# A transformer block kernel: eight modulation blocks on VectorE, two routing operations moved, three idle products

## The chip, the cores and the metric

The kernel runs on one core of a Trainium2 chip, in one launch. The time is the device time of that core in microseconds (us), as the median of several runs. TensorE (PE) multiplies matrices and writes PSUM; VectorE (DVE), ScalarE (ACT) and GpSimd (POOL) do the elementwise work; SyncE (SP) issues most of the transfers (DMA). Each engine works through its own queue in order.

## What is computed

Two transformer blocks, one behind the other, on 256 tokens of 1024 channels, in float32. The first takes its shifts, scales and gates from a conditioning row `c`; its token mixer adds three branches (attention, gated linear attention, Hyena), and its second half is a mixture of 16 experts. Cut to what matters here:

```
shift1, scale1, gate1, shift2, scale2, gate2 = split(silu(c) @ w_mod + b_mod, 6)
h = modulate(rms_norm(x), shift1, scale1)
m = sigmoid(g_hy) * (y_hy @ w_br_hy) + sigmoid(g_gla) * (y_gla @ w_br_gla) \
  + sigmoid(g_att) * (y_att @ w_br_att)
x = x + gate1 * (m @ w_out)
h = modulate(rms_norm(x), shift2, scale2)
scores = sigmoid(h @ router_w); sel = scores + router_b
...   # the best group of four experts by its two best, two experts in it
x = x + gate2 * grouped_moe(h)
```

`w_mod` has 1024 rows and 6 x 1024 columns. The change concerns how `gate1` and `shift2` are computed.

## The kernel before

**Weights.** They come from memory in the fixed order of `stream_order` (L249), about 1 MB at a time, into tiles `raw`; `load` (L512, L515) issues the transfers on SP as tiles come free. For most products a weight is split into a rounded high half, made by ACT, and the rest, the low half, made by DVE (`split`, L463, which writes `w`), both in the fast format fp32r; the product is then the sum of three matmuls (`mm3`). Tiles of 8 KB per partition, `raw`, `w` and `acc` of the change among them, share 19 buffers. `stream` keeps about three such halves ahead of the place where the next is taken.

**Order.** The program writes out each engine's order by hand. Beside the main line run side jobs (`Side`, L383): attention (`att`), gated linear attention (`glj`), Hyena (`hyj`) are generators, and `side.tick()` runs their next step when a planner's clock says that its operands are ready. That clock (`Clocked`, L341) adds a cost to PE, ACT or DVE for each call, so work that is added to or taken from an engine moves the steps behind it. All calls go through `Clocked.call`, so the profile gives them one line, L379.

**The modulation blocks.** `w_mod` comes in blocks of 128 rows by 2048 columns. Eight of them (shift and scale of the first half) are multiplied early; the other sixteen, blocks 0 to 15 in this document, are spread over the three branches. `mod_block` (L1354) is called in the loop over the gates of a branch (`w_brg`, four weights, each taken in two halves of 24 matmuls) and in the one over its projection (`w_br_...`). Blocks 0 to 3 lie in the gates of attention, 4 to 7 in its projection, 8 to 13 in the linear attention stage, 14 and 15 in the gates of Hyena. Blocks 0 to 7 add up to `gate1` and `shift2`, 8 to 15 to `scale2` and `gate2`. `mod_rows` (L815) multiplies a block with `cs`, which is `silu(c)` in the first of 32 columns and zero in the others, by four float32 matmuls (two instructions each) that write four groups of 32 rows of one PSUM bank `mod`:

```
for j in range(4):
    P.matmul(ps[32 * j:32 * j + 32], cs[:, k], w[:, 0, j * 512:j * 512 + 512], start=k == 0, stop=k == 7)
```

At a half's fifth block a tile `bm` is cleared by DVE and filled with `b_mod` by four transfers on ACT's queue; at its eighth, DVE adds the bank to it. The generator `mod_spread` (L1389) then splits it into `mrow`, spreads each row over the 128 partitions with eight matmuls against `pick` (32 rows), and ACT copies the results into `mod2`. For the first half it also turns `shift2` with eight transposes (`turned_half`) and multiplies it with the router's weights (`shifted`). One step of it is made in each of the next blocks.

**The attention steps** on PE turn the weights of the softmax (`c_base,e`), make the next scores (`kT,qT`) and weigh the values (`pT,kv`); ACT copies `pT` and makes `e`, DVE makes the maxima `nb`, scales `e` and makes the low half of the result `ya`. `uc` are the columns of Hyena's short convolution, of which each has an ACT and a DVE operation.

**Routing** (from L1575). When `w_out` has been multiplied, the second half's input `h` is made for two tiles of 128 tokens. `high(m)` rounds it on ACT into `h2H`, `low(m, n)` takes the rest into `h2L`, in halves of 512 columns: for the first tile on DVE, for the second on POOL, right behind `high(1)`. DVE meanwhile makes `sel`, and by comparisons (`ge`, `gt`, `cnt`, `top`, `gs`, `cg`) the `mask` of experts. Four products of `mask` (eight instructions) count tokens per expert; `residual(i)` puts `x1` into four banks `pa` by a product with the identity matrix (`c_base` in the rows). The largest count, `mosti`, is loaded by all engines for a branch (L1695, L1696) that is not taken in these runs. Behind it `gather` makes the one-hot matrix `dp` and collects the experts' tokens, from `h2H` and then `h2L`. The stage of the experts follows.

Of the kernel before, what the change touches and what calls it, by code (L numbers as in the profile page):

```python
# [18 lines left out]
D = 1024  # L19
# [400 lines left out]
def program(ctx, tc, A, out, dump=None):  # L420
# [929 lines left out]

    acc2, mod2, spreads = {}, [], []

    def mod_block(i):

        hf, k = divmod(i, 8)
        w = take("mod2", i)
        if hf:
            next(spreads[0], None)
        if k == 0:
            acc2[hf] = PS("mod")  # L1360
        mod_rows(w, k, acc2[hf])
        if k == 4:
            st["bm"] = bm = T([128, 512], "bm", tag="u4")
            V.memset(bm, 0.0)
            for j in range(4):
                S.dma_start(bm[32 * j:32 * j + 1], A["b_mod2"][:, hf * 2048 + j * 512:hf * 2048 + j * 512 + 512])
        if k == 7:
            bm = st["bm"]
            V.tensor_tensor(bm, acc2.pop(hf), bm, op=OP.add)
            spreads.append(mod_spread(st.pop("bm")))  # L1370
            if False:
                next(spreads[hf])

# [10 lines left out]
    def logits(ts, ps, start, stop):  # L1384

        for k in range(8):
            P.matmul(ps, ts[k // 4][:, k % 4 * 128:k % 4 * 128 + 128], rw[:, k], start=start and k == 0, stop=stop and k == 7)

    def mod_spread(rows):  # L1389

        rH, rL = T2([128, 512], "mrow")
        split(rH, rL, rows)
        yield
        for a in range(2):
            t = T([128, D], "mod2")
            for n in range(2):
                ps = PS()
                q = slice(32 * (2 * a + n), 32 * (2 * a + n) + 32)
                P.matmul(ps, pick[q], rH[q], start=True, stop=False)
                P.matmul(ps, pick[q], rL[q], start=False, stop=True)  # L1400
                S.activation(t[:, n * 512:n * 512 + 512], ps, AF.Copy)
            mod2.append(t)
        yield
        if len(mod2) == 2:
            ts = [turned_half(mod2[1], k4) for k4 in range(2)]
            yield
            ps = PS()
            logits(ts, ps[:, :16], True, True)
            st["shifted"] = T([128, 16], "shifted", tag="uh")
            V.tensor_copy(st["shifted"], ps[:, :16])  # L1410

    msum = mH = mL = None
# [133 lines left out]

    def low(m, n, eng=V):
        c = slice(n * 512, n * 512 + 512)
        eng.tensor_tensor(h2[1][:, m, c], h2s[m][:, c], h2[0][:, m, c], op=OP.subtract)

# [20 lines left out]
    for i in range(1, 3):  # L1571
        residual(i)
    low(0, 0)
    h2H, h2L = h2
# [14 lines left out]
    high(1)  # L1589
    for n in range(2):  # L1590
        low(1, n, G)
    sel = R(E3, "sel")
# [103 lines left out]
    with tc.If(full > CAP, label="full"):  # L1696
# [11 lines left out]
        for e in range(N_EXP):  # L1708
# [27 lines left out]
            for m in range(2):  # L1736
                for n in range(2):
                    V.tensor_tensor(hfs[m], gu[n, m], gate2[:, n * 512:n * 512 + 512], op=OP.mult)
                    P.matmul(pa[m][n], ident, hfs[m], start=False, stop=False)

    next(first)
    next(first)
# [4 lines left out]
    gated, hids, done = {}, {}, {}  # L1747
    low, high = slice(0, 64), slice(64, 128)

# [9 lines left out]
    def gate_up(e, i, ps):  # L1759

        w = take("moe_gu", 4 * e + i)
        for k in range(2):
            x = xgs[e // 4][i // 2][:, (2 * i + k) % 4, e % 4]
            for a, q in enumerate((low, high)):
                P.matmul(ps[q], x, w[k][:, a * 512:a * 512 + 512], start=i + k == 0, stop=i + k == 4)
# [17 lines left out]
    def down(g):  # L1783
# [7 lines left out]
        for i in range(2):  # L1791
            if not (last and i):
                ws = [take("moe_down", 4 * g + 2 * a + i) for a in range(2)]
            for k, n in ((k, n) for n in range(2) for k in range(2)) if last and i else ((k, n) for k in range(2) for n in range(2)):
                if last and i and not k:
                    wn = take("moe_down", 4 * g + 1 + 2 * n)
                for a, q in enumerate((low, high)):
                    w = wn[a][:, k * 512:k * 512 + 512] if last and i else ws[a][k][:, n * 512:n * 512 + 512]
                    P.matmul(ps[n][q], hid[:, a, 2 * i + k], w, start=i + k == 0, stop=i + k == 2)
# [562 lines left out]
```

## Time and profile before

| | |
|---|---|
| median of 3 runs | 1410.7 us (1408.94 to 1415.88) |
| profiled execution | 1408.6 us, its span 1406.8 us |
| busy, share of span | PE 97%, DVE 60%, ACT 45%, POOL 1% |
| granted TensorE clock, mean | 0.993 |
| transfers | 297.4 MB, 211 GB/s over the span |

The profile is of one execution. Busy times are sums over instructions; matmuls are pipelined and overlap, so the time of a group is read from the starts of the groups around it. PEclk is the granted share of PE's full clock. An idle time stands before the instruction that ended it, with what released it.

### The profile page before, as it was taken

The page shows a single profiled execution, that of the slowest core. Times are in us where ns is not written, and L with a number is a line of the kernel's source. Part 1 is how long each engine was busy: PE and PEld are TensorE (multiplying, and loading weights), DVE is VectorE, ACT ScalarE, POOL GpSimd, SP SyncE. Part 2 cuts the span into 40 slices and gives each one's busy share as a digit, 9 for nine tenths or more (in the row PEclk, how much of TensorE's full clock was granted, in tenths as well). Part 3 has the DMA queues.
Part 4 walks back from the last instruction along what each step waited for, and adds up shares of the span by engine and source line. Part 5 has one row for each costly group of instructions (what it writes and reads, how often), then busy time and mean ns, then how long its engine had stood idle before and what let it go on. Part 6 is the DMA issues. An engine that isn't in the chain of part 4 may idle for free.

```text
span 1406.8 us, 20329 instructions
## 1 busy us (share of the span) xinstructions
PE 1359.7 (97%) x8270; PEld 1056.6 (75%) x8270; DVE 839.6 (60%) x1515; ACT 632.6 (45%) x1013; POOL 8.3 (1%) x15
## 2 busy tenths in 40 slices
PE   5999999999999899999999999999999998999998
PEld 2678889878797444343488689999978887999996
DVE  4777457445876511111365885666676788566675
ACT  4643465634433311111257644555435663555541
POOL 0000000000000000000000000000000000000000
PEclk9999999999999999999999999999999999999999
DMA  9523344635469799999842355556453354555630
GB/s 372 225 71 120 150 150 150 242 134 180 170 211 359 288 422 420 421 421 421 342 180 90 120 175 185 180 180 214 176 175 125 128 180 150 180 180 183 220 136 30
DMA packets 44481, 297.40 MB, mean 211 GB/s; under 512 B 5171, under 2 KB 6371, under 8 KB 10017
## 3 DMA queue, kind: packets, MB, share of 16 engines
q1 hardware_dynamic: 41868, 291.02, 55.3%
q10 hardware_dynamic: 1924, 3.27, 0.7%
q0 software_dynamic: 592, 1.79, 0.5%
q8 instruction: 66, 1.08, 0.3%
q14 instruction: 31, 0.25, 0.0%
HBM read 295.00 MB, written 1.05 MB: 210 GB/s over the span
## 4 chain that ended last, share of the span: by engine, by line
PE 56%; DVE 6%; ACT 2%; issue 1%; ACTq 0%; DVEq 0%
PE ps L379 47%; PE pd L379 8%; DVE w L379 2%; PE pa L379 1%; DVE v L379 1%; ACT pe L379 1%; DVE rs L379 1%; PE oc L379 1%; DVE xL L379 0%; DVE sm L379 0%; PE pq L379 0%; ACT w L379 0%; DVE bs L379 0%; DVE rsa L379 0%; ACT xH L379 0%
## 5 line engine op out<-in xcount | busy, mean ns | idle before, releaser
L379 DVE TENSOR_TENSOR w<-raw,w 128x1024 fp32r<-128x1024 f32 (+3 forms) x301 | 346.2, 1195 | 82.8 <-ACT w L379 82.1
L379 ACT ACTIVATE w<-raw 128x1024 fp32r<-128x1024 f32 (+3 forms) x301 | 293.1, 1032 | 17.2 <-PE ps L379 9.9
L379 PE MATMUL ps<-xH,w 128*128 128x256 f32 x1408 | 256.5, 283 | 0.3 <-ACT xH L379 0.3
L379 PEld LDWEIGHTS ps<-xH,w 128*128 128x128 f32 x1408 | 220.6, 192 | 1.5 <-ACT xH L379 0.8
L379 PE MATMUL ps<-xL,w 128*128 128x256 f32 x704 | 199.3, 283 | 1.1 <-DVE xL L379 1.1
L379 PE MATMUL ps<-w,xH 128*128 128x512 f32 (+2 forms) x544 | 150.3, 362 | 2.6 <-ACT xH L379 2.1
L379 PEld LDWEIGHTS ps<-xL,w 128*128 128x128 f32 x704 | 134.9, 192 | 2.2 <-DVE xL L379 1.5
L379 PE MATMUL pd<-w,fh 128*128 128x512 f32 x528 | 125.6, 394 | 0.0
L379 PE MATMUL ps<-raw,xg 128*64 128x512 f32 x512 | 120.0, 600 | 0.0
L379 PE MATMUL ps<-hH,w 128*128 128x256 f32 (+1 forms) x608 | 115.7, 287 | 0.0
L379 PEld LDWEIGHTS pd<-w,fh 128*128 128x128 f32 x528 | 98.2, 188 | 21.6
L379 PEld LDWEIGHTS ps<-w,xH 128*128 128x128 f32 x544 | 95.3, 189 | 18.0 <-ACT xH L379 4.0
L379 PEld LDWEIGHTS ps<-hH,w 128*128 128x128 f32 (+1 forms) x608 | 94.9, 187 | 7.9 <-issue 2.7
L379 PE MATMUL ps<-w,xL 128*128 128x512 f32 (+2 forms) x272 | 97.8, 359 | 1.9 <-DVE xL L379 1.8
L379 PE MATMUL ps<-w,hH 128*128 128x512 f32 (+1 forms) x288 | 88.1, 390 | 0.0
L379 PE MATMUL ps<-hL,w 128*128 128x256 f32 (+1 forms) x304 | 85.9, 282 | 0.0
L379 PEld LDWEIGHTS ps<-raw,xg 128*64 128x64 f32 x512 | 33.3, 136 | 55.7 <-issue 52.6
L379 DVE SCALAR_TENSOR_TENSOR fc<-ps,par,fc 128x255 f32<-128x255 f32 x88 | 42.5, 483 | 51.8 <-ACT fc L379 50.2
L379 ACT ACTIVATE fc<-ps,par 128x256 f32<-128x256 f32 x44 | 24.8, 564 | 92.5 <-PE ps L379 66.6
L379 PEld LDWEIGHTS ps<-w,hH 128*128 128x128 f32 x288 | 52.2, 188 | 13.8 <-issue 2.7
L379 PEld LDWEIGHTS ps<-w,xL 128*128 128x128 f32 x272 | 51.3, 188 | 11.9 <-DVE xL L379 5.0
L379 PE MATMUL ps<-raw,hid 128*64 128x512 f32 x256 | 57.4, 593 | 0.1
(443 smaller groups left out, 1845.5 us busy)
## 6 DMA issues: line engine op xcount, KB each, us to landing
raw<-in_moe_gu SPq DMA_DIRECT2D x63, 1024.0 KB, 14.3
raw<-in_moe_down SPq DMA_DIRECT2D x32, 1024.0 KB, 13.5
raw<-in_mod SPq DMA_DIRECT2D x24, 1024.0 KB, 5.0
raw<-in_ffn_gate SPq DMA_DIRECT2D x22, 1024.0 KB, 4.8
raw<-in_ffn_up SPq DMA_DIRECT2D x22, 1024.0 KB, 5.0
raw<-in_ffn_down SPq DMA_DIRECT2D x22, 1024.0 KB, 4.9
raw<-in_w_brg SPq DMA_DIRECT2D x12, 1024.0 KB, 5.9
raw<-in_ple_gate SPq DMA_DIRECT2D x8, 1024.0 KB, 5.6
```

The costliest lines, as they stand in the source:

```text
L379: return f(*args, **kw)
```

## The change

Three things are changed.

1. Blocks 0 to 7 are added up on DVE. A tile `acc` of 128 x 2048 is cleared by DVE, its first row filled with `b_mod` by one transfer on ACT's queue, and for each block two operations add `raw` times the column of `cs`, 1024 columns each. `mod_sums` then splits `acc` into two pairs of `mrow` tiles and sums over the partitions with eight matmuls against `ones` (128 x 128, made once by ACT), which also spread the sum. Its steps, the turning of `shift2` and `shifted` among them, are made in blocks 8 to 13. The bank `mod` and `bm` of the first half fall away.
2. `low(1, n)` goes from POOL to DVE, and behind the branch.
3. Three products of `ident` and `x1` into a bank `idle` that nobody reads stand on PE between `residual(2)` and the products of `mask`.

The new names `left` and `right` for two slices change nothing.

```diff
+    ones = T([128, 128], "pick", F32R)
+    S.activation(ones, C("ones16"), AF.Copy, scale=16.0)
...
         w = take("mod2", i)
-        if hf:
-            next(spreads[0], None)
+        if not hf:
+
+            if k == 0:
+                st["acc"] = acc = T([128, 2048], "acc")
+                V.memset(acc, 0.0)
+                S.dma_start(acc[0:1], A["b_mod2"][:, :2048])
+            acc = st["acc"]
+            for n in range(2):
+                c = slice(n * 1024, n * 1024 + 1024)
+                V.scalar_tensor_tensor(acc[:, c], w[:, 0, c], cs[:, k, 0:1], acc[:, c], op0=OP.mult, op1=OP.add)
+            if k == 7:
+                spreads.append(mod_sums(st.pop("acc")))
+            return
+        next(spreads[0], None)
         if k == 0:
             acc2[hf] = PS("mod")
         mod_rows(w, k, acc2[hf])
...
+    def mod_sums(acc):
+
+        for a in range(2):
+            rH, rL = T2([128, D], "mrow")
+            split(rH, rL, acc[:, a * D:a * D + D])
+            yield
+            t = T([128, D], "mod2")
+            for n in range(2):
+                ps = PS()
+                for r in (rH, rL):
+                    P.matmul(ps, ones, r[:, n * 512:n * 512 + 512], start=r is rH, stop=r is rL)
+                S.activation(t[:, n * 512:n * 512 + 512], ps, AF.Copy)
+            mod2.append(t)
+            yield
+        ts = [turned_half(mod2[1], k4) for k4 in range(2)]
+        yield
+        ps = PS()
+        logits(ts, ps[:, :16], True, True)
+        st["shifted"] = T([128, 16], "shifted", tag="uh")
+        V.tensor_copy(st["shifted"], ps[:, :16])
...
-    def low(m, n, eng=V):
+    def low(m, n):
         c = slice(n * 512, n * 512 + 512)
-        eng.tensor_tensor(h2[1][:, m, c], h2s[m][:, c], h2[0][:, m, c], op=OP.subtract)
+        V.tensor_tensor(h2[1][:, m, c], h2s[m][:, c], h2[0][:, m, c], op=OP.subtract)
...
     for i in range(1, 3):
         residual(i)
+
+    idle = PS("idle")
+    for i in range(3):
+        P.matmul(idle, ident, x1[:, 0, :512], start=True, stop=True)
     low(0, 0)
...
     high(1)
-    for n in range(2):
-        low(1, n, G)
...
+    for n in range(2):
+        low(1, n)
     next(first)
     next(first)
```

**Order on DVE in the gates of attention, at the first block.** `w` are low halves of weights, `nb` and `ya` belong to an attention step. Before:

```order
L379 TENSOR_TENSOR w_1326<-raw_1262,w_1326 128x1024
L379 TENSOR_TENSOR w_1354<-raw_1262,w_1354 128x1024
L379 TENSOR_TENSOR ya_1417<-ps_1412,ya_1417 128x256
L379 TENSOR_REDUCE nb_1420<-ps_1404 128x1
...
L379 TENSOR_REDUCE nb_1423<-ps_1408 128x1
```

With the change:

```order
L379 TENSOR_TENSOR w_1328<-raw_1264,w_1328 128x1024
L379 TENSOR_TENSOR w_1356<-raw_1264,w_1356 128x1024
L379 MEMSET acc_1361 128x2048
L379 SCALAR_TENSOR_TENSOR acc_1361<-raw_990,cs_105,acc_1361 128x1024 x2
L379 TENSOR_TENSOR w_1393<-raw_1366,w_1393 128x1024
L379 TENSOR_TENSOR ya_1446<-ps_1441,ya_1446 128x256
L379 TENSOR_REDUCE nb_1449<-ps_1433 128x1
```

The memset and two products now stand between two low halves, and one more low half comes before the attention step.

**Order on PE at the end of attention.** `pT,kv` weighs the values, `c_base,e` turns the softmax, `ya,w` is the projection, `mod` a block. Before:

```order
L379 MATMUL ps_2118<-c_base_80,e_1894 128x128 x4
L379 MATMUL ps_2124<-c_base_80,e_1897 128x128 x4
L379 MATMUL ps_2130<-pT_2001,kv_592 128x256 x4
L379 MATMUL ps_2147<-hH_315,w_1973 128x256
...
L379 MATMUL ps_2207<-pT_2117,kv_592 128x256 x4
L379 MATMUL ps_2214<-ya_1417,w_2060 128x256 x6
...
L379 MATMUL ps_2214<-ya_2135,w_2088 128x256 x6
L379 MATMUL mod_1359<-raw_1941,cs_105 32x512 x4
```

With the change:

```order
L379 MATMUL ps_2124<-c_base_80,e_1879 128x128 x4
L379 MATMUL ps_2130<-c_base_80,e_1882 128x128 x4
L379 MATMUL ps_2136<-pT_1981,kv_592 128x256 x4
...
L379 MATMUL ps_2183<-c_base_80,e_2016 128x128 x4
L379 MATMUL ps_2189<-c_base_80,e_2019 128x128 x4
L379 MATMUL ps_2195<-pT_2123,kv_592 128x256 x4
L379 MATMUL ps_2203<-pT_2182,kv_592 128x256 x4
L379 MATMUL ps_2210<-ya_1446,w_2032 128x256 x6
...
L379 MATMUL ps_2210<-ya_2200,w_2060 128x256 x6
L379 MATMUL ps_2283<-ya_1446,w_2095 128x256 x6
```

The two weigh products at the end have no matmuls of weights between them any more, and the block behind the first 48 projection matmuls is gone.

**Order on PE in routing.** `pa` is a residual. Before:

```order
L379 MATMUL pa_4185<-x_3956,c_base_80 128x512
L379 MATMUL pa_4187<-x_3956,c_base_80 128x512
L379 MATMUL ps_4222<-mask_4219,c_base_80 128x32
L379 MATMUL ps_4222<-mask_4219,c_base_80 128x16 x3
L379 MATMUL pa_4227<-x_3956,c_base_80 128x512
```

With the change:

```order
L379 MATMUL pa_4169<-x_3940,c_base_80 128x512
L379 MATMUL pa_4171<-x_3940,c_base_80 128x512
L379 MATMUL idle_4173<-x_3940,c_base_80 128x512 x3
L379 MATMUL ps_4208<-mask_4205,c_base_80 128x32
L379 MATMUL ps_4208<-mask_4205,c_base_80 128x16 x3
L379 MATMUL pa_4213<-x_3940,c_base_80 128x512
```

The idle products stand between the third residual and the mask, and the last residual stays behind the mask.

## Rows read from the trace of the kernel before

**Rows 1.** The page's part 1: busy time, share of span and instructions of each engine.

```profile
PE 1359.7 (97%) x8270; PEld 1056.6 (75%) x8270; DVE 839.6 (60%) x1515; ACT 632.6 (45%) x1013; POOL 8.3 (1%) x15
```

**Rows 2.** Table by stage: window, length, busy us (instructions) per engine, PEclk, DMA share, GB/s.

```profile
180.00:195.00 15.00, 15.00 (x103) 13.09 (x102) 5.61 (x11) 7.06 (x13) 0.00 (x0) 1.00 0.61 220
225.00:240.00 15.00, 15.00 (x118) 14.64 (x117) 11.97 (x19) 8.96 (x14) 0.00 (x0) 1.00 0.44 146
255.00:270.00 15.00, 15.00 (x99) 11.27 (x99) 6.05 (x8) 8.73 (x12) 0.00 (x0) 1.00 0.54 188
```

**Rows 3.** Timeline, routing: start us, length us, engine, line, op, out<-in, count, [idle before].

```profile
464.22 1.96 PE L379 MATMUL pa<-x,c_base 128*128 128x512 f32 x4
...
467.04 2.48 POOL L1549 TENSOR_TENSOR h2L<-h,h2H 128x512 fp32r<-128x512 f32 x2 [54.05 <-ACT h2H L379]
467.19 1.15 DVE L379 SCALAR_TENSOR_TENSOR top<-cnt,sel 128x32 f32<-128x32 f32 x1
...
468.60 0.97 DVE L379 TENSOR_TENSOR ge<-gs 128x32 f32<-128x32 f32 x1
469.49 0.18 DVE L379 TENSOR_TENSOR gt<-gs 128x32 f32<-128x32 f32 x1
...
470.58 1.86 PE L379 MATMUL ps<-mask,c_base 128*128 128x32 f32 x8 [4.40 <-DVE mask L379]
...
472.28 2.05 PE L379 MATMUL pa<-x,c_base 128*128 128x512 f32 x2
...
474.64 1.91 PE L379 MATMUL ps<-dp,h2H 128*128 128x256 f32 x8 [0.30 <-PEq L1696]
```

**Rows 4.** Table by stage, routing; columns as in group 2.

```profile
468.00:469.00 1.00, 0.00 (x0) 0.00 (x0) 0.93 (x3) 0.00 (x0) 1.00 (x2) 1.00 1.01 426
469.00:470.00 1.00, 0.00 (x0) 0.00 (x0) 0.93 (x4) 0.00 (x0) 0.52 (x1) 0.72 0.95 401
471.00:473.00 2.00, 2.00 (x8) 1.76 (x9) 0.49 (x5) 0.00 (x0) 0.00 (x0) 0.50 0.03 12
```

**Rows 5.** Timeline of PE in the gates of attention, 190 to 199 us.

```profile
191.19 1.64 PE L379 MATMUL ps<-kT,qT 128*128 128x512 f32 x6
...
197.15 0.28 PE L379 MATMUL ps<-hH,w 128*128 128x256 f32 x1
197.35 1.07 PE L379 MATMUL mod<-raw,cs 128*32 128x512 f32 x8
198.35 0.38 PE L379 MATMUL ps<-hH,w 128*128 128x256 f32 x1
```

**Rows 6.** Timeline of PE in the attention branch's projection, 253 to 258 us.

```profile
253.74 1.06 PE L379 MATMUL mod<-raw,cs 128*32 128x512 f32 x8
254.73 3.11 PE L379 MATMUL ps<-ya,w 128*128 128x256 f32 x24
```

**Rows 7.** View of tile `mod`: operation, count: ns min/median/max, first and last start, form.

```profile
L379 DVE SCALAR_TENSOR_TENSOR mod<-mod,g2n x1: 1226/1226/1226, 446.0 to 446.0; 128x1024 f32<-128x1024 f32 x1
```

**Rows 8.** Groups on DVE, 160 to 316 us: busy us, mean ns, idle before them.

```profile
L379 DVE TENSOR_TENSOR w<-raw,w 128x1024 fp32r<-128x1024 f32 x31 | 37.6, 1223 | 19.8 <-ACT w L379 19.8
...
L379 DVE TENSOR_REDUCE nb<-ps 128x1 f32<-128x512 f32 x12 | 8.2, 682 | 2.6 <-PE ps L379 2.6
...
L379 DVE TENSOR_TENSOR ya<-ps,ya 128x256 fp32r<-128x256 f32 x8 | 3.4, 423 | 18.6 <-ACT ya L379 18.6
...
L379 DVE MEMSET att<- 128x1024 f32 x1 | 0.9, 912 | 0.2 <-issue 0.2
```

**Rows 9.** View of tile `mrow`; columns as in group 7.

```profile
L379 PE MATMUL ps<-mrow,pick x16: 383/442/497, 314.0 to 444.5; 32*128 32x512 f32 x16
```

**Rows 10.** Timeline of ACT at the end of attention.

```profile
246.35 0.56 ACT L379 ACTIVATE uc<-ps,par 128x256 f32<-128x256 f32 x1 [1.38 <-PE ps L379]
247.99 0.56 ACT L379 ACTIVATE uc<-ps,par 128x256 f32<-128x256 f32 x1 [1.07 <-DVE uc L379]
...
252.26 2.01 ACT L379 ACTIVATE w<-raw 128x1024 fp32r<-128x1024 f32 x2 [3.44 <-DMA wa<-in_ba]
```

More of the change, by code (lines that the diff above doesn't have):

```diff
@@ L1370, in mod_block @@
             spreads.append(mod_spread(st.pop("bm")))
-            if False:
-                next(spreads[hf])
     rw = Pc("router_w").rearrange("p (k e) -> p k e", k=8)
@@ L1403, in mod_spread @@
         yield
[L1404 to L1410, printed above, removed]
     msum = mH = mL = None
@@ L1747, in program @@
     gated, hids, done = {}, {}, {}
-    low, high = slice(0, 64), slice(64, 128)
+    left, right = slice(0, 64), slice(64, 128)
     def load_p(i):
@@ L1763, in gate_up @@
             x = xgs[e // 4][i // 2][:, (2 * i + k) % 4, e % 4]
-            for a, q in enumerate((low, high)):
+            for a, q in enumerate((left, right)):
                 P.matmul(ps[q], x, w[k][:, a * 512:a * 512 + 512], start=i + k == 0, stop=i + k == 4)
@@ L1796, in down @@
                     wn = take("moe_down", 4 * g + 1 + 2 * n)
-                for a, q in enumerate((low, high)):
+                for a, q in enumerate((left, right)):
                     w = wn[a][:, k * 512:k * 512 + 512] if last and i else ws[a][k][:, n * 512:n * 512 + 512]
```

## The prediction

> **What bounds the kernel now.** I began with the busy shares: TensorE (PE) works for 97% of the span [rows 1]. A change helps here if it takes work out of PE's queue, or shortens one of PE's few waits. Then the table by stage, for the stretch in which blocks 0 to 7 lie, about 160 to 285 us: PE is busy in every microsecond at the full granted clock, while VectorE (DVE) is busy 5.61 of 15 us in one slice, 11.97 in another and 6.05 in a third [rows 2]. Work can go from PE to DVE there, but DVE has no room for any amount of it. Last the waits: PE's longest between 150 and 480 us is 4.40 us for `mask` during routing [rows 3]. In the same rows GpSimd (POOL) makes the two low halves from 467.04 to 469.52, and two small DVE operations of the chain to `mask` take far longer than their like: `top` 1.15 and the second `ge` 0.97 us, where `gt`, with `ge`'s operands, takes 0.18 [rows 3]. PE did nothing from 466.18; the granted clock was 1.00 up to 469, 0.72 in the next microsecond and then 0.50 (1.2 of 2.4 GHz) [rows 4]. What follows runs at half rate: eight mask instructions in 1.86 us and the first eight of the gather in 1.91 [rows 3].
>
> **The change, part by part.** The sum is made against the profiled execution's 1408.6 us. The median of the three runs, 1410.7, is 2.1 higher, and I add that at the end.
>
> *Eight blocks leave PE.* Each is eight instructions of which four run side by side. The matmul before a block starts at 197.15 and the one behind it at 198.35; one such step is 3.11/24 = 0.13 us [rows 6], so a block takes 1.20 - 0.13 = 1.07 [rows 5]. In the later stage it is 254.73 - 253.74 = 0.99 [rows 6]. Four of each are 8.2, with the slow first matmul behind a block some 8.5. Bounds 7.9 and 9.4: **-8.5**.
>
> *DVE gets sixteen products.* The nearest row is a SCALAR_TENSOR_TENSOR of 128x1024 float32 with 1.226 us [rows 7]; sixteen are 19.6. The memset of 128x2048 costs twice the 0.91 of 128x1024 [rows 8], 1.8. The first product then waits for the one-row transfer of `b_mod`, which is issued behind that memset; the nearest row is ACT's wait of 3.44 us for a small transfer of the same queue [rows 10], so 0 to 3.4. Is there cover? Between the gates of the attention stage come eight weight splits (8 x 1.22 [rows 8]), eight products and about 2.7 attention steps of some 3.5 us (one `ya` of 0.42 and two `nb` of 0.68 [rows 8], the rest two scalings of `e`, half a microsecond each, and small ones): 9.8 + 9.8 + 9.4 = 29 us of DVE. PE has 8 x 24 matmuls, 24 of them in 3.05 us [rows 6], and 2.7 steps of about 3, so 32. DVE fills nine tenths of PE's time, and the memset and the wait, at most 5.2 together, come on top. The code splits weights three halves ahead of PE, 3 x 3.05 = 9 us, and that lead bears it. DVE's idle time before its weight splits and before `ya`, 19.8 + 18.6 us over 156 [rows 8], is where the new work goes. I cost it at **0**. If the lead is used up, what is late next is the low half of a weight, and PE waits.
>
> *Sums over partitions.* Eight matmuls of 32 rows, 442 ns each [rows 9] but up to four at a time, give way to eight of 128 rows. Six matmuls of 512 columns at the same rate take 1.64 us [rows 5]; eight then take about 2.0, and the old ones between 0.8 and 1.7: **+0.7**, between +0.3 and +1.2. The two wider splits (two of about 1.0 on ACT [rows 10], two of 1.22 on DVE [rows 8]) lie beside matmuls.
>
> *Side steps move.* The planner's clock no longer counts the blocks, so attention, GLA and Hyena steps fall elsewhere. At the end of attention two weigh products now follow each other, and the second needs two `pT` copies which ACT reaches only behind two `uc` operations. Before, that pair took from 246.35 to 248.55, the second waiting for DVE [rows 10]; with two copies of 512 columns, about 0.5 each by the 2.01 for two of 1024 [rows 10], the operand is there some 3.5 us after the matmuls that release the first `uc`, and PE is free after about 1.6. I take **+1.9**, between 0 and 3. In GLA the wider evacuations stand ahead of its copies on ACT: **+0.5**, between 0 and 1.5. Everything up to `w_out`: -8.5 + 0.7 + 1.9 + 0.5 = **-5.4**.
>
> *Routing.* With POOL out of it, `top` and `ge` fall to about 0.19 and 0.18: 0.96 + 0.79 = **-1.75** on the chain to the mask, which is then ready about 468.7. The three idle products are six instructions; four take 1.96 us, about 0.43 a step [rows 3], so they run from 465.94 to about 468.5, just ahead of the mask, and hold up nothing. PE then never rests for long, so the mask's instructions take half of 1.86, **-0.9**, and the first gather gains about **-0.7** of its 1.91 [rows 3]. The gather started at 474.64, just 0.31 after the third residual, which took 2.05 at half rate [rows 3]; should the residual have held it, and not the branch ahead of it, up to 0.6 more is gained, and I take **-0.3**. Routing: -3.6, between -1.7 and -4.3. The low halves on DVE behind the branch are two of some 0.7 us (from 1.22 for 1024 columns [rows 8]) beside the first gather's products and cost nothing; were that cover gone, at most 1.4. The MoE stage behind it is full of transfers whose start is set by the same branch, so it moves as a whole.
>
> Sum: -5.4 - 3.6 = -9.0, so 1399.6 for an execution like the profiled one and 1401.7 against the median; I say **1402**.
>
> *Two rules against the rows.* The rows show `top` and `ge` slow while POOL works, and normal once it has ended. The Trainium skill, SBUF — State Buffer, on the pair of ports that DVE and GpSimd share, says that of a DVE instruction with two SBUF inputs and a GpSimd instruction that reads SBUF the second to start waits until the first has ended. By that rule 1.05 and 0.92 us were waits, and the term would be about -2.0 instead of -1.75. On the clock, the rows show it full for almost 3 us after PE's last product, and then half. The Trainium skill, TensorE: Matmul & The Clock Gate, Part 1, says that the throttled state is the default and that the same kernel showed different counts of slow matmuls from run to run. By that rule the gap that remains ahead of the gather (the residual would end about 470.8, the gather begin about 471.7) could still cost the clock; that is the second rival, and no row here shows it for so short a gap.
>
> **The rivals.**
>
> 1. *DVE becomes the bound; slower.* The products stand in order ahead of weight splits, and attention steps wait for PE and ACT in between. If DVE's idle time can't be filled, because it only marks when ACT delivers, all of 19.6 + 1.8 + 3.4 = 24.8 us come into line: -9.0 + 24.8 = +15.8, or 1426; with half of it +3.4, or 1414. From 9 us of new PE waits on the change loses, from 16 on by more than 0.5%. For it: the nine tenths above, and the 11.97 of 15 us [rows 2]. Against it: the lead of three halves, and that the stage behind it has DVE busy for 6.05 of 15 us [rows 2].
> 2. *The clock falls anyway, or the idle products end behind the mask.* Then the 0.9, 0.7 and 0.3 are gone: -7.1, or 1403.6. For it: the products end within 0.2 us of the mask. Against it: clock 1.00 through 468 to 469 after nearly 3 us without work [rows 4].
> 3. *The lead runs out in part.* Single waits of PE for splits, in the attention stage or where the hyena columns keep DVE busy for 11.97 of 15 us [rows 2], of 3 to 6 us together: 1405 to 1408. `acc` also holds one of the 19 buffers of its size through the whole stage, which can only bring weights later.
> 4. *The blocks' time was not PE's.* If the stream of weights sets the pace of this stage, their 8.5 us turn into waits for it, and only routing is left: -3.6, or 1407. Against it: PE's slices are full [rows 2], without gaps that would show such a pace.
>
> **How the numbers follow.** A measurement of this kernel can tell about 0.5%, 7 us, from no change. My forecast has 0.46, with 1398 to 1403.6; a better case, without the two stalls of the moved steps (-11.4, or 1399, and down to 1396 with the upper bounds of the blocks and of routing), 0.07. The second rival has 0.10 and sits on the bound, so half of it counts as faster by more than 0.5%. The third has 0.20, the fourth 0.09; the first has 0.08. So faster 0.46 + 0.07 + 0.05 = 0.58, which I cut to 0.54 for the forecast's own spread over the bound; same 0.38; slower 0.08. The range is 1396 to 1409: it leaves out the first rival and the tails.
>
> **What the profile should show.** In the stretch from 160 to 285 us no `mod` group on PE, and two DVE products of 1.2 us per block; PE's waits there under 3 us, most of them for `pT` at the end of attention; the end of the mask's products some 8 us earlier than before (5.4 + 1.75 + 0.9). `top` and `ge` at about 0.2 us, PE's wait for `mask` under 0.5, the granted clock at 1.00 through the gather. I am wrong if PE waits for low halves of weights by more than 5 us, if the products take much over 1.23, if the idle products end well behind the mask, or if the clock is at 0.50 during the mask's products.

## The result, and the profile after

The changed kernel takes 1400.09 us in the median of five runs (1396.86 to 1400.38), against 1410.7 (1408.94 to 1415.88): a ratio of 0.991, with a 95% interval of 0.989 to 0.9931. That is 10.6 us faster where 8.7 were forecast (1402).

PE's share is the same, with 58 matmul instructions fewer (the page's part 1, where [rows 1] stood):

```profile
PE 1354.2 (97%) x8212; PEld 1054.8 (75%) x8212; DVE 860.9 (62%) x1533; ACT 634.5 (45%) x1015; POOL 5.8 (0%) x13
```

Where the time went is best read from first starts in PE's timeline, since, apart from falls of the clock, a stretch between two of them comes out alike in every profile of the same instructions, to 0.1 us in the stages of the change and to 0.4 in the start (e6_double_products below is 1.3 longer there). The stretches are: the start, up to the first scores of attention (`kT,qT`); attention's gates (up to the first `ya,w`); the rest of the three branches (up to the first `w,mH` of `w_out`); routing, from there to the first product of an expert (`raw,xg`); the experts and half of the second block (up to the first `w,ycH`); and the end. In brackets stands the clock that was lost, the sum of one minus the granted clock over the stretch, in us. It says that the clock fell, not what that cost: the kernel before lost 1.7 us in its start, and its start is no longer than those that lost nothing (138.24 to 138.52).

| kernel | start | gates | rest of the branches | routing | experts and on | end |
|---|---|---|---|---|---|---|
| before | 138.10 (1.7) | 109.59 (0) | 184.72 (0) | 46.94 (3.4) | 664.48 (0) | 262.96 (4.5) |
| changed | 143.06 (5.1) | 106.45 (0) | 181.46 (1.7) | 43.35 (0) | 664.36 (0) | 259.76 (0.5) |

Gates and the rest are 6.40 us shorter, routing 3.59. The start is 4.96 longer and the end 3.20 shorter, with not one instruction changed in either: there the clock fell at other moments, of which more below. So the two profiles differ by 8.4 us in span, and the stretches that the change touches by 10.0.

In the attention stage DVE is now busy for 13.54 of 15 us at the most, in the slice where [rows 2] had 5.61 (the stage begins 5 us later in this span, so the slices do not hold quite the same work), and in the slices shown PE still has no gap (the table by stage, columns as there):

```profile
180.00:195.00 15.00, 15.00 (x116) 14.53 (x116) 13.54 (x23) 7.89 (x14) 0.00 (x0) 1.00 0.59 222
195.00:210.00 15.00, 15.00 (x116) 14.53 (x116) 12.19 (x20) 13.17 (x18) 0.00 (x0) 1.00 0.52 201
255.00:270.00 15.00, 15.00 (x108) 13.00 (x107) 8.62 (x11) 7.62 (x10) 0.00 (x0) 1.00 0.61 226
```

The view of the tile `acc` gives the new work its price (ns min/median/max; the last line is DVE's idle time ahead of it, us and times):

```profile
L379 DVE SCALAR_TENSOR_TENSOR acc<-raw,cs,acc x16: 1271/1279/1285, 176.5 to 285.2; 128x1024 f32<-128x1024 f32 x16
...
L379 DVE MEMSET acc<- x1: 1765/1765/1765, 172.9 to 172.9; 128x2048 f32 x1
...
  DMA acc<-in_b_mod: 1.9, 1
```

And the groups of DVE from 160 to 316 us, the window of [rows 8] (busy us, mean ns, idle before them), show what it filled: the idle time before the low halves of weights and before `ya`, 19.8 and 18.6 us in [rows 8], is 13.3 and 4.4:

```profile
L379 DVE TENSOR_TENSOR w<-raw,w 128x1024 fp32r<-128x1024 f32 x34 | 41.2, 1221 | 13.3 <-ACT w L379 13.2
L379 DVE SCALAR_TENSOR_TENSOR acc<-raw,cs,acc 128x1024 f32<-128x1024 f32 x16 | 19.8, 1278 | 1.9 <-DMA acc<-in_b_mod 1.9
...
L379 DVE TENSOR_TENSOR ya<-ps,ya 128x256 fp32r<-128x256 f32 x8 | 3.4, 423 | 4.4 <-ACT ya L379 4.4
```

At the end of attention the second weigh product waits for its `pT`, as the step on moved work had it (timeline, PE and ACT):

```profile
244.81 1.89 PE L379 MATMUL ps<-pT,kv 128*128 128x256 f32 x8
...
246.28 0.56 ACT L379 ACTIVATE uc<-ps,par 128x256 f32<-128x256 f32 x1 [1.69 <-DVE uc L379]
246.74 1.07 ACT L379 ACTIVATE pT<-ps 128x512 f32<-128x512 f32 x2
...
247.87 1.59 PEld L379 LDWEIGHTS ps<-pT,kv 128*128 128x128 f32 x8 [1.57 <-ACT pT L379]
```

The second wait was not foreseen. In the linear attention stage the second low half of the sums stands on DVE behind two low halves of weights, and PE waits 2.30 us for it (timeline, DVE and PE):

```profile
344.73 2.35 DVE L379 TENSOR_TENSOR w<-raw,w 128x1024 fp32r<-128x1024 f32 x2
...
345.49 0.47 PE L379 MATMUL ps<-mrow,pick 128*128 128x512 f32 x1
...
347.00 1.22 DVE L379 TENSOR_TENSOR mrow<-acc,mrow 128x1024 fp32r<-128x1024 f32 x1
...
348.27 0.96 PE L379 MATMUL ps<-mrow,pick 128*128 128x512 f32 x3 [2.30 <-DVE mrow L379]
```

In this execution the clock fell 1.2 us behind that wait (table by stage):

```profile
349.00:350.00 1.00, 1.00 (x10) 0.16 (x8) 1.00 (x3) 0.89 (x2) 0.00 (x0) 0.75 0.93 393
350.00:351.00 1.00, 1.00 (x5) 0.26 (x2) 1.00 (x2) 0.86 (x1) 0.00 (x0) 0.50 1.08 451
351.00:352.00 1.00, 1.00 (x6) 1.00 (x7) 0.68 (x1) 0.99 (x2) 0.00 (x0) 0.50 0.94 369
```

Routing, where [rows 3] stood (timeline):

```profile
464.58 2.74 PE L379 MATMUL idle<-x,c_base 128*128 128x512 f32 x6
...
465.75 0.19 DVE L379 SCALAR_TENSOR_TENSOR top<-cnt,sel 128x32 f32<-128x32 f32 x1
...
466.20 0.19 DVE L379 TENSOR_TENSOR ge<-gs 128x32 f32<-128x32 f32 x1
...
467.32 1.07 PE L379 MATMUL ps<-mask,c_base 128*128 128x32 f32 x8
...
468.23 1.10 PE L379 MATMUL pa<-x,c_base 128*128 128x512 f32 x2
...
470.26 1.29 DVE L379 TENSOR_TENSOR h2L<-h,h2H 128x512 fp32r<-128x512 f32 x2 [0.66 <-DVEq L1723]
...
470.32 1.19 PE L379 MATMUL ps<-dp,h2H 128*128 128x256 f32 x8 [0.99 <-DVEq L1723]
...
471.35 1.12 PE L379 MATMUL ps<-dp,h2L 128*128 128x256 f32 x8
```

`top` and the second `ge` take 0.19 us, the mask's eight instructions 1.07 instead of 1.86, the first gather 1.19 instead of 1.91. The idle products end at 467.32, 0.06 us behind the mask on DVE, and the mask's products start at once. The low halves (470.26, two in 1.29 us) lie beside the gather's first products, and the second group starts without a wait.

### The profile page after: what moved, and what is told of

It is laid out like the page before. It is cut to its first block, busy times and chain, and to the rows that moved or that the text cites. A ratio compares the mean times of both kernels' runs of the same rounds, so it can differ in the third digit from the quotient of the medians.

```text
span 1398.4 us, 20223 instructions
## 1 busy us (share of the span) xinstructions
PE 1354.2 (97%) x8212; PEld 1054.8 (75%) x8212; DVE 860.9 (62%) x1533; ACT 634.5 (45%) x1015; POOL 5.8 (0%) x13
## 3 DMA queue, kind: packets, MB, share of 16 engines
q8 instruction: 65, 1.06, 0.3%
HBM read 295.00 MB, written 1.05 MB: 212 GB/s over the span
## 4 chain that ended last, share of the span: by engine, by line
PE 56%; DVE 6%; ACT 2%; DMA 1%; issue 1%; ACTq 0%; SPq 0%; DVEq 0%
PE ps L379 46%; PE pd L379 8%; DVE w L379 2%; DVE v L379 1%; PE pa L379 1%; ACT pe L379 1%; DVE rs L379 1%; DMA raw<-in_ab_q 1%; PE oc L379 1%; DVE xL L379 0%; DVE sm L379 0%; PE pq L379 0%; ACT w L379 0%; DVE bs L379 0%; DMA pt<-in_p 0%
```

## The experiments

Each run below was made with a profile, and timed beside the kernel before on the same chip.

| run | start | gates | rest of the branches | routing | experts and on | end | median us | ratio (95%) |
|---|---|---|---|---|---|---|---|---|
| e1_blocks_only | 138.39 (0) | 106.46 (0) | 181.44 (1.7) | 47.01 (3.4) | 664.30 (0) | 262.64 (4.2) | 1400.67 | 0.9933 (0.991 to 0.9956) |
| e2_routing_only | 138.28 (0) | 109.60 (0) | 186.17 (1.7) | 43.37 (0) | 665.89 (1.7) | 261.63 (2.9) | 1409.35 | 0.998 (0.9962 to 0.9998) |
| e3_no_idle | 143.37 (6.8) | 106.45 (0) | 181.43 (1.7) | 45.83 (3.4) | 664.43 (0) | 262.16 (4.7) | 1399.41 | 0.9916 (0.9898 to 0.9934) |
| r2_no_idle | 143.25 (6.8) | 106.45 (0) | 181.40 (1.7) | 45.84 (3.4) | 665.89 (1.7) | 259.79 (0.8) | 1397.82 | 0.9897 (0.9878 to 0.9916) |
| r4_no_idle | 143.38 (6.8) | 106.46 (0) | 179.88 (0) | 45.68 (3.4) | 664.26 (0) | 259.77 (0.7) | 1399.3 | 0.9916 (0.9894 to 0.9938) |
| r1_changed | 138.37 (0) | 106.44 (0) | 181.45 (1.7) | 43.31 (0) | 664.31 (0) | 259.74 (0.5) | 1397.9 | 0.9918 (0.9891 to 0.9945) |
| r3_changed | 138.49 (0) | 106.44 (0) | 179.87 (0) | 43.34 (0) | 664.35 (0) | 262.63 (4.3) | 1398.43 | 0.9908 (0.9889 to 0.9926) |
| e4_pool_low | 138.52 (0) | 106.44 (0) | 181.45 (1.7) | 46.40 (1.7) | 664.27 (0) | 259.77 (0.7) | 1402.43 | 0.9942 (0.992 to 0.9964) |
| e6_double_products | 144.72 (6.8) | 112.48 (0) | 181.32 (0) | 43.42 (0) | 664.33 (0) | 262.71 (4.2) | 1406.34 | 0.9964 (0.995 to 0.9977) |
| e5_splits_first | 138.51 (0) | 106.45 (0) | 183.01 (3.4) | 44.82 (1.7) | 664.24 (0) | 261.34 (2.9) | 1400.09 | 0.9929 (0.9907 to 0.9951) |
| e9_sum_later | 138.24 (0) | 106.44 (0) | 183.37 (3.4) | 44.82 (1.7) | 664.32 (0) | 261.30 (3.0) | 1400.92 | 0.9918 (0.9892 to 0.9944) |
| e8_busy_waits | 143.25 (6.8) | 106.42 (0) | 183.43 (3.4) | 44.82 (1.7) | 664.39 (0) | 259.71 (0.5) | 1402.0 | 0.993 (0.9913 to 0.9947) |

**The two halves of the change, each alone.** The first has the blocks on DVE, and neither the idle products nor the moved low halves; the second is the kernel before with these two only:

```diff
-    idle = PS("idle")
-    for i in range(3):
-        P.matmul(idle, ident, x1[:, 0, :512], start=True, stop=True)
...
+    for n in range(2):
+        low(1, n, G)
```

> The kernel before with part 1 alone (blocks 0 to 7 on DVE). Theory: the two parts of the gain are independent, and the stretch from the first attention step to the first product of w_out is 6.4 us shorter, as in the changed kernel (there -1.44 at w_out after +4.96 at the start of attention); the routing stretch from w_out to the gather is as before (clock 0.50 at the mask, top and ge about 1 us). The time falls by 5 to 8 us. Rival: the gain of this part was luck of the clock; then the stretch differs from -6.4 by over 2 us.

> The kernel before with parts 2 and 3 alone (low halves on DVE behind the branch, three idle products). Theory: the stretch from the first product of w_out to the second group of the gather is 3.6 us shorter, all stages ahead of it are as before, the clock is at 1.00 at the mask and in the gather; the time falls by 2.5 to 5 us. Rival: without the earlier part the idle products end behind the mask or the branch comes no earlier; then the stretch is under 2 us shorter.

For the stretches both theories hold to a tenth of a microsecond. With the blocks alone gates and rest take 287.90 us, 6.41 less than before, and routing 47.01. With routing alone that stretch is 43.37, 3.57 less, and the gates 109.60. In these stretches the parts neither help nor hinder each other. Neither median lies where it was expected. That of the first is 10.0 us below the kernel before (1410.63), where 5 to 8 were expected. That of the second is only 1.3 below, where 2.5 to 5 were expected: its twelve executions form two groups, six from 1403.8 to 1407.0 and six from 1411.7 to 1412.6, and the median falls in the gap between them. What set the groups apart is not known; the profile is one of the lower group, and even it lost 1.7 us of clock in each of two stretches where the profile of before lost none.

**Without the idle products.** The changed kernel less the three products:

> The changed kernel without the three idle products. Theory: PE then has no work for about 2.7 us ahead of the mask, the clock falls as before, and mask products and first gather run at half rate: about 1.7 us more (0.9 for the mask's products, 0.7 to 0.9 for the gather). Rival: the shorter chain alone keeps the clock up, the granted clock stays at 1.00 until the gather, and the routing stretch is the changed kernel's within 0.3 us.

> The changed kernel without the three idle products, again. Theory: PE is without work for about 2.7 us ahead of the mask; the clock falls there or at the gather in most executions, 2 to 3.5 us, so the median is 1 to 3 us above the changed kernel's on the same chip. Rival: the medians are within 1 us, so the idle products bring nothing that the time shows.

> The kernel without idle products a third time: does the clock fall at the mask, at the gather or at both. Theory: in at least two of its three profiles the routing stretch (first product of w_out to first expert's product) is 2 us or more above the changed kernel's 43.35 us. Rival: in at most one.

> The changed kernel again, beside the one without idle products on the same chip. Theory: PE's wait ahead of the mask is 0.8 us and the clock never falls there; in the gap of 1 us ahead of the gather it falls in some executions, at a cost of about 1.5 us; so this profile may show the gather at 1.03 us for its first group or at 1.6 to 1.9. The waits for the second low half of the sums (2.3 us) and in the second block cost the clock in some executions and not in others. Rival: in the changed kernel the clock stays up through the gather in every profile.

> The changed kernel a third time, for the same question: does the clock fall ahead of the gather or not (first group 1.03 us or more), and which of the other waits cost it this time. Theory and rival as in the run of it ahead of this one.

In three profiles of three the routing stretch is 2.3 to 2.5 us longer than in three of the changed kernel (45.68 to 45.84 against 43.31 to 43.35). That is what was expected of r4_no_idle, and more than the 1.7 us expected of e3_no_idle. But only once did the clock fall at the mask, as the theory had it. In r4_no_idle the mask's products are slow (timeline of PE):

```profile
466.14 1.74 PE L379 MATMUL ps<-mask,c_base 128*128 128x32 f32 x8 [2.67 <-DVE mask L379]
...
470.07 2.05 PE L379 MATMUL ps<-dp,h2H 128*128 128x256 f32 x8 [0.30 <-PEq L1720]
```

In the other two the mask's products run at full rate, though PE has waited 2.66 us, and the clock falls only in the residual behind them (468.41 to 469.67), so that the gather's first two groups take 2.04 and 1.91 us (r2_no_idle, timeline of PE, then the table by stage):

```profile
467.53 1.04 PE L379 MATMUL ps<-mask,c_base 128*128 128x32 f32 x8 [2.66 <-DVE mask L379]
...
470.50 2.04 PE L379 MATMUL ps<-dp,h2H 128*128 128x256 f32 x8 [0.83 <-DVEq L1720]
472.35 1.91 PE L379 MATMUL ps<-dp,h2L 128*128 128x256 f32 x8
```

```profile
469.00:470.00 1.00, 0.67 (x2) 0.00 (x0) 0.76 (x2) 0.00 (x0) 0.00 (x0) 0.62 0.00 0
```

So in the changed kernel the idle products do hold up the clock: without them it falls ahead of the gather in two profiles of three and at the mask in one. The rival written for r1_changed and r3_changed holds for the changed kernel itself, whose three profiles show a clock of 1.00 through the gather; but in e5, e8 and e9 below, with the same instructions there, it fell 0.2 to 0.3 us behind the start of the gather. So they do not hold it up in every version. For the time the rival written for r2_no_idle holds, that the medians are within 1 us: 1399.04 over the 19 executions without the idle products, 1398.51 over the 17 with them. The falls elsewhere vary by more than these 2.4 us; whether routing loses them in every timed execution as well stays open.

**The low halves back on GpSimd.** The changed kernel with the line `low(1, n, G)` behind `high(1)` again:

> The changed kernel with the second token tile's low halves back on GpSimd, the idle products kept. Theory: top and the second ge take about 1 us again, the mask comes 1.7 us later than in the changed kernel, PE waits for it some 2.5 us instead of 0.8, at a clock that stays at 1.00, so the gather is 1.7 us later. Rival 1: the wait of 2.5 us costs the clock too, then 3 to 3.5 us later. Rival 2: GpSimd was not what slowed top and ge; then nothing moves.

The timeline (POOL, DVE and PE) shows `top` and `ge` slow again while POOL's two operations run, from 461.02 to 463.51:

```profile
461.02 2.49 POOL L1574 TENSOR_TENSOR h2L<-h,h2H 128x512 fp32r<-128x512 f32 x2 [54.03 <-ACT h2H L379]
461.18 1.16 DVE L379 SCALAR_TENSOR_TENSOR top<-cnt,sel 128x32 f32<-128x32 f32 x1
...
462.59 0.97 DVE L379 TENSOR_TENSOR ge<-gs 128x32 f32<-128x32 f32 x1
...
464.48 1.06 PE L379 MATMUL ps<-mask,c_base 128*128 128x32 f32 x8 [1.74 <-DVE mask L379]
```

PE waits 1.74 us for the mask, which comes 1.72 us later in its stretch than in the changed kernel (38.07 us from the first `w,mH` against 36.35). That wait was expected at 2.5. The clock then falls in the gap ahead of the gather, and routing takes 46.40, 3.05 more: rival 1. Of the 3.59 us of routing, the move of the low halves is thus worth 1.7 on the chain to the mask, and the remaining 1.3 of the 3.05 belong to the clock, which fell in this execution and not in those of the changed kernel. This run puts the low halves back both onto GpSimd and ahead of the branch. `top` and `ge` each end 0.05 us behind an operation of POOL (462.34 and 463.56, against 462.29 and 463.51), which speaks for the engine; low halves on DVE ahead of the branch, or on GpSimd behind it, were not run.

**How near DVE was to setting the pace.** A second product behind each of the sixteen:

```diff
                 V.scalar_tensor_tensor(acc[:, c], w[:, 0, c], cs[:, k, 0:1], acc[:, c], op0=OP.mult, op1=OP.add)
+                junk2 = T([128, 1024], "twice", tag="u4")
+                V.engine.scalar_tensor_tensor(junk2, w[:, 0, c], cs[:, k, 0:1], w[:, 0, c], op0=OP.mult, op1=OP.add)
```

> The changed kernel with a second product of the same size behind each of the sixteen on DVE, into a tile that nobody reads; the planner's clock does not count it, so the order is the changed kernel's. It measures how near DVE was to setting the pace. Theory (DVE filled nine tenths of PE's time in the gates of attention and had half its time free behind them): 9.8 us more of DVE against 3 us free and a lead of 9 us; PE waits 0 to 6 us between the start of attention and the first product of the projection (106.45 us in the changed kernel), and not in the projection. Rival 1: DVE was the bound already; then nearly all of it shows, 9 us or more in the gates. Rival 2: DVE had room for twice the work; then under 0.5 us.

The gates take 112.48 instead of 106.45 us, 6.03 more, at the theory's upper end. PE's waits (us in total, times, longest) say what came late, not a weight but the scaled softmax, in the order of the same engine, and `kw` in the stage behind:

```profile
PE ps L379 <- DVE sm L379: 5.0, 3, 2.2
...
PE ps L379 <- DVE kw L379: 1.0, 1, 1.0
```

So of 10.2 us of added work in the gates (eight of 1.280) about 4 were hidden. The rest of the branches, without a fall of the clock, takes 181.32 us where r3_changed takes 179.87, so the doubled products cost 7.5 us in all; the median is 7.8 above the 1398.51. Eight products are the work of four blocks, and four blocks on PE cost 4.8 (half of the 9.6 measured for eight, below). The changed kernel uses up most of the room that DVE had in the gates; by these prices, four more blocks there would have lost more than they bring. This is the first rival's case: it begins not far behind the change.

The same run also answers for the wait of 2.30 us. It is there, and the clock behind it stays at 1.00 (timeline of PE, then the table by stage):

```profile
357.40 0.96 PE L379 MATMUL ps<-mrow,pick 128*128 128x512 f32 x3 [2.30 <-DVE mrow L379]
```

```profile
358.00:359.00 1.00, 1.00 (x10) 0.16 (x8) 1.00 (x3) 1.00 (x2) 0.00 (x0) 1.00 0.89 360
359.00:360.00 1.00, 1.00 (x10) 0.71 (x7) 1.00 (x3) 0.75 (x2) 0.00 (x0) 1.00 1.03 434
```

**Can the wait for the sums be had back?** Two tries. One makes both splits ahead of the first products, the other puts an empty step in front of the second products:

```diff
-        for a in range(2):
-            rH, rL = T2([128, D], "mrow")
+        rows = [T2([128, D], "mrow") for _ in range(2)]
+        for a, (rH, rL) in enumerate(rows):
             split(rH, rL, acc[:, a * D:a * D + D])
             yield
+        for rH, rL in rows:
             t = T([128, D], "mod2")
```

```diff
             split(rH, rL, acc[:, a * D:a * D + D])
             yield
+            if a:
+                yield
```

> The changed kernel with both splits of the sums made in the first two steps, ahead of the first products with ones. Theory: PE's wait of 2.30 us for the second low half of the sums came from the low half standing behind a chain of small operations on DVE; made a step earlier it is there in time, the wait goes and with it the fall of the clock behind it, which cost 1.7 us: the stretch from the start of attention to w_out is 3 to 4 us shorter than 287.9. Rival: PE then waits for the next low half of a weight instead, and the stretch is within 1 us of 287.9.

> The changed kernel with one more empty step between the second split of the sums and its products, so that the second products with ones stand 48 projection matmuls and a block later on PE. Theory: the low half is long there, PE's wait of 2.30 us goes and with it the fall of the clock that sometimes followed; the stretch from the start of attention to w_out, 287.9 us with the fall and 286.3 without, becomes about 284, and the median falls by 2 to 3 us below the changed kernel's 1398.5 (17 executions). Rival 1: as in the splits-first version another operand is late in its place (the gate of the linear attention branch, or the Hyena steps that the moved order delays), and the stretch stays above 286. Rival 2: the wait for the projection's own operand, which stood behind the same DVE chain, takes over the 2.3 us at the same place.

Neither works, and both times another operand is late instead. With the splits first, ACT makes the rounded half (1.06 us) ahead of the `qkT` copies that the next step of linear attention needs; its rival had looked for a low half of a weight. With the sums later, PE runs into the next operand of the same DVE chain, the low half of `yg`, as the second rival had it. PE's waits in the one and the other:

```profile
PE ps L379 <- ACT qkT L379: 1.9, 1, 1.9
```

```profile
PE ps L379 <- DVE yg L379: 3.0, 1, 3.0
```

Both lost 3.4 us of clock in that stretch, twice as much as the changed kernel's profile, so they come out at 289.5 and 289.8 us, longer than its 287.9. With 1.6 us taken off for each 1.7 of clock (the difference between r1_changed and r3_changed) all three are at 286.3 to 286.6: nothing is gained, and nothing lost but to the clock. In both tries it is the chain on DVE and ACT that ends last, and PE's saved time is partly given back to it.

**Products in more of PE's waits.** The splits-first version with a helper that writes products into a bank nobody reads, three ahead of the first transposes, one and two in the second block:

```diff
+    def busy(r, n):
+        t = PS("idle")
+        for _ in range(n):
+            P.engine.matmul(t, ident, r, start=True, stop=True)
```

> The splits-first version with idle products in three more of PE's waits: three at the start ahead of the transposes of x (a wait of 2.7 us), one ahead of the last attention's transposes in the second block (2.2 us) and two ahead of its last low half (2.0 us). Theory: these waits cost the clock in some executions and not in others (the stretch behind the experts' stage lost between 0.5 and 4.7 us so, the start 0 to 6.8); with products in them the clock stays up there, and the median falls by 1 to 4 us below that of the splits-first version, with a smaller spread. Rival: the falls at the start come from its sparse products and not from that wait, and the products in the waits delay what is waited for; then the median is the same within 1 us.

The median is 1402.0, 1.9 above the splits-first version's 1400.09. So the theory fails; the rival, which had the same median within 1 us, is not met either, but its account of the start fits. At the start the clock fell as far as it ever does (6.8 us lost) although PE had work in the wait of 2.7 us. In the end stretch only 0.5 us were lost, but so it was in two of three profiles of the changed kernel, so nothing follows from that. The spread is smaller than that of the splits-first version, as expected (4.4 against 6.8 us, six executions each), but the changed kernel's own sets of five and six spread by 3.3 to 9.6. No version tried is clearly faster than the changed kernel, whose three sets have medians of 1400.09, 1397.9 and 1398.43.

## Why the prediction was right

*What bounds the kernel, and the eight blocks: -8.5.* The sign and the place were right, the size a little short. In r3_changed, a profile whose branches lost no clock, the `mod` groups take 7.97 us less, start to next start, between the first scores and `w_out`, and the matmuls of `hH` and `ya`, which stood ahead of and behind the blocks, 1.6 less: -9.6, just outside the bounds of 7.9 to 9.4. In the profile before, the matmul of `hH` or `ya` ahead of such a block takes 0.21 us to the next start and the one behind it 0.22, where the others take 0.12. I had counted the one ahead for four blocks only and allowed 0.3 in all for those behind.

*Sixteen products on DVE at 0.* Right. They take 1.279 us instead of the 1.226 of [rows 7], the memset 1.77 and the wait for `b_mod` 1.9, within the 0 to 3.4. In the attention stage PE waited for no low half. (The 3.05 us that I read from [rows 6] for 24 matmuls stands there as 3.11; nothing hangs on it.) That the cover was there but mostly used up, "nine tenths of PE's time", is what the doubled products showed.

*Sums over partitions: +0.7.* The eight new matmuls take 2.58 us and the old ones 1.38, so +1.2, at the upper bound. *Moved steps: +1.9 and +0.5.* The place of the first was right, the size over: the wait is 1.17, because PE was busy for 2.9 us behind the matmuls that release the first `uc`, with `c_base,e` (243.82, 1.15 us) and the first weigh product (to 246.70), where I had assumed 1.6; the operand itself came 4.0 us behind them, where I had 3.5, as DVE released the second `uc` only at 246.28. The second was the term most out of size. PE waits 2.30 us for `mrow` and 0.3 for `S`, and two waits of 0.4 and 0.5 are gone: +1.7, above the 1.5 that I had as its upper bound, and I had looked for it on ACT, with the copies of `mod`, where it stood on DVE. The clock's fall behind it added 1.6 in six of the nine profiles with this wait (not in r3_changed, r4_no_idle and e6_double_products). Against it stand 1.7 us that I had not seen: PE's waits for `z` and `YL` in the Hyena stage became shorter with the moved order (PE's waits, us in total, times, longest, before and then in r3_changed, which has none for `YL`):

```profile
PE ps L379 <- ACT z L379: 1.1, 1, 1.1
...
PE ps L379 <- DVE YL L379: 0.8, 1, 0.8
```

```profile
PE ps L379 <- ACT z L379: 0.2, 1, 0.2
```

*Everything up to `w_out`: -5.4.* Measured -6.4 in the execution compared, and -8.0 without the clock's fall (r3_changed). The measured terms, -9.6 + 1.2 + 1.2 + 1.7 - 1.7, make -7.2; the other 0.8 is spread over groups that the moved order shifted, and I can't name its cause. That -6.4 lies so near to -5.4 is in part luck: the fall of the clock, which I had not priced, took back 1.6 of a gain that was larger than forecast.

*Routing: -3.6.* Measured -3.59. The mask's products start 1.82 us earlier (-1.75), the time from there up to the start of the gather is 1.06 shorter (4.06 to 3.00; -0.9 and -0.3), the gather's first group 0.72 (1.75 to 1.03; -0.7). Of the 1.06, 0.27 lie behind the start of the last residual, the prediction's third (2.36 to 2.09 us from there to the gather), near the 0.3 that I took and not the 0.6 that I allowed at most. On DVE alone, from the start of `top` to that of `mask`, the chain takes 1.32 instead of 3.06 us: 1.74 shorter, as the rows had it. By the estimate from the rule of the Trainium skill on the ports that DVE and GpSimd share (SBUF — State Buffer, SBUF: two separate sides), the chain would have gained 2.0 (its first wait is 1.1 by [rows 3], not 1.05, which leaves the 2.0 as it is). The trace agrees with the rule in where the slow operations end, 0.05 us behind an operation of POOL in e4_pool_low, but not with the 2.0: an operation that takes 0.19 us by itself has only 0.05 left when POOL has ended, so the whole wait was not gained.

*The second rival* was right about the place. At the gather (0.4 us ahead of it in e4, 0.2 to 0.3 behind its start in e5, e8 and e9) the clock fell with the idle products kept, at 1.3 to 1.5 us where the rival had 1.9, while the changed kernel's three profiles and two others show 1.00 there. *The fourth* is excluded by e1: PE's time in this stage became the kernel's time. *The third* did not happen in the attention stage; its form in the linear attention stage is the wait of 2.30 us.

What I did not price at all is the clock outside the changed places. It cost the changed kernel's profile 4.96 us at the start against that of before and gave 3.20 back at the end. The medians hold such falls on both sides, and whether they cancel there no run shows. The three sets of the changed kernel have medians 10.6, 12.8 and 12.2 us below the kernel before timed with them, so the 8.7 that I forecast was 2 to 4 us too small, and in r3_changed's profile what was too small lies ahead of `w_out`: -8.0 where I had -5.4.

## What to carry to other kernels

Read a stage's room from the engine that receives the work, over the very stretch between two places where it must deliver, and count its order: here DVE, busy for 5.61 of 15 us in one slice, looked empty, and one more product for each of the moved ones cost 7.5 us. Where work moves from the bounding engine into a chain of small operations, ask which operand of that chain is next to be late, since in two tries out of two putting the late one elsewhere only passed the wait on. Compare two profiles by stretches between first starts of the same instruction, with the lost clock beside each; a total alone would have hidden both a loss of 5 us and a gain of 3 that no edit made.

## What the runs showed of the hardware

The same wait of PE costs the clock in one execution and not in the next. The wait of 2.30 us for `mrow` was followed by a fall in the changed kernel's first two profiles and by none in its third, nor in e6_double_products, with the same instructions around it. The start, which no kernel but e8 changes, lost nothing in seven profiles and up to 6.8 us in six; from 30 to 32 us into it, two executions of the changed kernel (table by stage):

```profile
30.00:32.00 2.00, 2.00 (x3) 0.96 (x4) 1.25 (x2) 1.90 (x1) 0.06 (x1) 0.50 1.01 422
```

```profile
30.00:32.00 2.00, 2.00 (x6) 0.94 (x5) 1.60 (x2) 1.60 (x1) 0.36 (x1) 1.00 1.00 418
```

In the stretches shown, but for the last, a fall lost 1.7 us of clock, or up to four times that (6.8 at the start of e6_double_products). The Trainium skill, TensorE: Matmul & The Clock Gate, Part 1, says that the count of slow matmuls varies from run to run, and these rows agree. For this kernel it means that one execution lies up to 8 us from another (the kernel before: 1408.5 to 1416.3 us in 59 of them) with nothing changed, and that gains below that are to be read by stretch.
